# Element-wise transfers replaced by TensorE transposes, and two side streams with further waiting steps, in a two-layer hybrid decoder step

## Chip, core and metric

The kernel runs on one core of one Trainium2 chip. The metric is device time in microseconds (us) of one execution; the time before is 2325.03 us, the median of three runs.

## The reference

Two groups of tokens pass through a 2-layer decoder with shared weights: a prompt of 2048 tokens and 8 sample rows of one token each, all 1024 wide, in f32. A layer is

```
hn   = RMSNorm(x) * norm_w
proj = hn @ w_in                      # 1024 x 3336, split into 15 column groups
A retention      : r_q r_k r_v r_g    # 4 heads, state 64 x 64, rotary on q and k
B mLSTM          : m_q m_k m_v m_o m_g m_i m_f    # state c, n, m
C S5             : s_u s_g            # 16 groups, 64 complex states each, x_t = a x_(t-1) + B u_t
D memory attend  : a_q a_g            # 256 memory tokens
y    = x + concat(A, B, C, D, each times a SiLU gate) @ w_out
```

A final RMSNorm follows. The last states of A, B and C are outputs for both groups. For the S5 states these are `s5re_p`, `s5im_p` (16 x 64 per layer) of the prompt and `s5re_s`, `s5im_s` of the samples.

## The kernel before

**Units.** The 2048 tokens are cut into 4 units of 512 (UT), so there are 8 units, (layer, unit) from (0,0) to (1,3). `wstream` (L277) lists the work as weight groups: per unit 13 groups of 256 columns of w_in (`m_v` with 8 more), and the four output groups `out0` to `out3` of the unit before. The order is ORDER (L41): m_v, s_u, out0 to out3, m_k, m_q, m_o, a_q, r_k, r_v, r_q, s_g, a_g, m_g, r_g. In unit (0,1) the outputs stand behind a_q. Each f32 product is three float32r products (a value split into a high and a low part), so weights are loaded, split on ScalarE and on VectorE or GpSimd (`wsplit`, L345), and kept split in DRAM (`ws`) for the next units.

**Main stream and sides.** `group` (L449) is a Python generator for one weight group. It emits a piece of matmuls into a PSUM bank, evacuates it, and yields. At each yield `step_sides` (L1854) lets every side stream in `self.sides` emit up to its own next yield. So a bare `yield` in a side stream is a waiting step: its next instructions are emitted one main piece later. Tile's scheduler fixes each engine's order from this at build time; at run time an engine takes its instructions in that order. Almost all DMAs are issued on SyncE's queue by `dma` (L190), some on ScalarE's by `dmaa` (L193), where ScalarE's own later work stands behind them.

**Samples.** The 8 sample rows ride in unit 1 of each layer. Seven groups, FEAT (L37), are computed features by tokens: there the 8 sample columns are columns 512 to 519 of `hT`, a unit's 512 columns are cut into pieces of 260, and the result for the samples is 128 features by 8 rows. Lines 479 to 481 copy it to a small tile and store it transposed into `sproj`, a DRAM buffer of 8 rows by 3336, so each element is a run of 4 bytes. The other groups go through `sample_group` (L1538), which writes rows. After `r_g` the side stream `sample_layer` (L1577) reads `sproj` back in the layouts that each branch wants. `sample_s5` (L1773) loads the inputs of S5 transposed again, element by element (L1785).

**The other lines concerned.** `s5_pre` (L1112) prepares the S5 tables of a layer; it loads `s5_a_re` and `s5_a_im` transposed, each twice (L1122, L1123), and B in four arrangements (L1129). For layer 0 it starts with the kernel, for layer 1 in unit (0,2). `s_core` (L1321) is the S5 scan of a unit; in the last unit it stores the final state transposed (L1392). `m_gates` (L804) makes the mLSTM gates: after its transposes it copies RT (L857), waits one step, copies a part of RT (L862) and multiplies it on TensorE (L863), and then sets G_done, for which `m_core` waits. `sample_hn` (L1520) loads the norm weights, normalises the 8 sample rows (ScalarE, then some 12 small VectorE instructions) and transposes them on TensorE. It is called inline: before the main loop for layer 0 (L1924), and at `out3` of layer 0 for layer 1 (L1564).

Of the kernel before, what the change touches and what calls it, by code (L numbers as in the profile page):

```python
# [22 lines left out]
SG = 16  # L23
# [5 lines left out]
D_IN = 3336  # L29
# [4 lines left out]
NB = 8  # L34
# [84 lines left out]
class Builder:  # L119
# [93 lines left out]
    def setup(self):  # L213
        nc, I, cp = self.nc, self.I, self.cp
        c = lambda n, s, dt=F32: cp.tile(s, dt, name=n, tag=n)
        self.ident = c("ident", [128, 128])
        self.dma(self.ident, I["c_ident"])
        self.wstream()
        self.mem_load()
        self.wload(0)  # L220
        self.hnl = self.hn_load(0, 0)
        next(self.hnl)
        self.wload(1)
        self.maskb = c("maskb", [128, 512], BF16)
        self.identb = c("identb", [128, 128], BF16)
        mt = self.t2([128, 512])
        self.dma(mt, I["c_mask"])
        nc.vector.tensor_copy(self.maskb, mt)
        nc.vector.tensor_copy(self.identb, self.ident)
        self.Dt = c("Dt", [128, 2, 2, 128])  # L230
        self.dma(self.Dt, I["c_D"])
        self.vd = c("vd", [128, H])
        self.dma(self.vd, I["c_vd"])
        self.ropes = c("ropes", [128, 2, 16])
        self.dma(self.ropes, I["c_ropes"])
        self.smc = c("smc", [128, 4])
        self.dma(self.smc, I["c_sm"])
        self.e127 = c("e127", [128, 1])
        self.dma(self.e127, I["c_e127"])
        self.s32 = c("s32", [128, 32])  # L240
        self.dma(self.s32, I["c_s32"])
        self.s8 = c("s8", [128, 8])
        self.dma(self.s8, I["c_s8"])
        st = self.t2([128, H])
        self.dma(st, I["c_sel"])
        self.sel = c("sel", [128, H], F32R)
        nc.vector.tensor_copy(self.sel, st)
        zero = self.t2([128, 320])
        nc.vector.memset(zero, 0.0)
        self.ones = c("ones", [128, 1])  # L250
        nc.vector.memset(self.ones, 1.0)

        self.hT = [cp.tile([128, 8, UT + NB], F32R, name=f"hT{i}", tag=f"hT{i}") for i in range(2)]
        self.Sr = [c(f"Sr{i}", [128, 2, 128]) for i in range(3)]
        self.Cm = [c(f"Cm{i}", [128, 2, 130]) for i in range(3)]
        for t in self.Sr + self.Cm:
            nc.vector.memset(t, 0.0)
        self.mprev = c("mprev", [4, 8])
        self.hS = [c(f"hS{i}", [128, 8, 40], F32R) for i in range(2)]
        for i in range(2):  # L260
            nc.vector.tensor_copy(self.hS[i].rearrange("p a b -> p (a b)"), zero)

        T = self.T
        self.xd = [self.dram([T, D], f"xd{i}") for i in range(self.depth)]
        self.xsd = [self.dram([NB, D], f"xsd{i}") for i in range(self.depth)]
        self.sproj = [self.dram([NB, D_IN], f"sproj{i}") for i in range(self.depth)]
        self.smix = [self.dram([NB, D], f"smix{i}") for i in range(self.depth)]
        self.stab = []
        self.memd = []
        for l in range(self.depth):  # L270
            self.stab.append(dict(
                Wi=self.dram([128, SG, 128], f"Wi{l}"), TW=self.dram([128, 3, 1024], f"TW{l}"),
                CS=self.dram([128, 2, SG, 128], f"CS{l}"), Kd=self.dram([32, 16, 112], f"Kd{l}"), ab=self.dram([128, 3, SG], f"ab{l}"),
                C1=self.dram([128, SG, SC], f"C1{l}")))
            self.memd.append((self.dram([128, 2, MEM], f"mk{l}"), self.dram([128, 2, GW], f"mv{l}")))
# [173 lines left out]
    def group(self, i):  # L449
# [5 lines left out]
        if kind == "mem":  # L455
            self.mem_group(l, b, hi, lo)
            self.advance(i, 0)
            self.advance(i, 1)
            yield
        elif kind == "out":  # L460
            if self.sample_in_unit(kind, l, b):
                while not self.smix_done[l]:
                    self.step_sides()
                self.sample_group(i, l, g, hi, lo, kind)
            yield from self.group_out(i, l, b, g, hi, lo)
        elif g in FEAT:
            if g == "r_q":
                for m in range(2):
                    self.u["rq", m] = self.g4([128, 2, UT], n="rqt")
                    self.dmaa(self.u["rq", m], self.I["c_rq"][b, m])  # L470
            smp = self.sample_in_unit(kind, l, b)
            pieces = [(0, 260), (260, 520)] if smp else [(0, UT)]
            for m in range(2):
                for c0, c1 in pieces:
                    ps = self.feat_bank(m, hi, lo, slice(c0, c1))
                    c2 = min(c1, UT)
                    self.evac_f(l, b, g, m, ps[:, :c2 - c0], slice(c0, c2))
                    if c1 > UT:
                        o = self.sm([128, 16])[:, :NB]
                        self.nc.vector.tensor_copy(o, ps[:, c2 - c0:c1 - c0])  # L480
                        self.dma(AP(self.sproj[l], COL[g] + 128 * m, [[1, 128], [D_IN, NB]]), o)
                    if (c0, m) == (0, 0):
                        self.advance(i, 0)
                    if c1 >= UT and m == 1:
                        self.advance(i, 1)
                    yield
        else:
            if g == "m_v":
                jobs = [[t] for t in range(4)]
            else:  # L490
                jobs = [[0, 1], [2, 3]]
            n = 264 if g == "m_v" else 256
            for m, ts in enumerate(jobs):
                sls = [slice(t * 128, (t + 1) * 128) for t in ts]
                ps = self.tok_bank(sls, n, hi, lo, self.hslice)
                self.evac(l, b, g, m, ps)
                if m in (0, len(jobs) - 1):
                    self.advance(i, min(m, 1))
                if g == "r_g":
                    nxt = self.next_unit(l, b)  # L500
                    if nxt:
                        self.hn_T(2 * m)
                        self.hn_T(2 * m + 1)
                yield
# [299 lines left out]
    def m_gates(self, u, l, b):  # L804
# [48 lines left out]
        ps = self.bank()  # L853
# [3 lines left out]
        v.tensor_copy(RT, ps.rearrange("p (t q h) -> p t q h", t=NT, q=4)[:, :, :, 0:H])  # L857
        u["RT"] = RT
        yield
        pw = self.bank()  # L860
        ws = self.sm([128, 16])
        v.tensor_copy(ws.rearrange("p (t h) -> p t h", t=NT), RT[:, :, 1, :])  # L862
# [249 lines left out]
    def s5_pre(self, l):  # L1112
# [5 lines left out]
        packA = self.t2([128, 512], n="packA")  # L1118
        packC = self.t2([128, 2, SG, SC], n="packC")
        ar, ai, dt = S(), S(), S()  # L1120
        for h in range(2):
            self.dma(ar[64 * h:64 * h + 64], I["s5_a_re"][l].rearrange("g p -> p g"))  # L1122
            self.dma(ai[64 * h:64 * h + 64], I["s5_a_im"][l].rearrange("g p -> p g"))  # L1123
        self.dma(dt, AP(I["s5_log_dt"][l], 0, [[0, 128], [1, SG]]))
        Bst = P1([2, SG, SC], "Bst")
        for h in range(2):
            for w in range(2):
                src = I["s5_b_re" if h == w else "s5_b_im"][l]
                self.dma(Bst[64 * h:64 * h + 64, w], src.rearrange("g p c -> p g c"))  # L1129
        yield  # L1130
        yield
        self.pexp(dt, SG)
        mag, th, cs, sn, k, tmp, thl = S(), S(), S(), S(), S(), S(), S()
        v.tensor_tensor(mag, ar, dt, OP.mult)
# [186 lines left out]
    def s_core(self, u, l, b):  # L1321
# [66 lines left out]
        yield  # L1388
        yield
        if b == self.NU - 1:  # L1390
            for h, on in enumerate(("s5re_p", "s5im_p")):
                self.dma(self.O[on][l, 0].rearrange("g p -> p g"), self.xprev[64 * h:64 * h + 64])  # L1392
        gl = self.g4([128, 2, UT], n="gl")
        gh_, gl_ = [self.g4([128, 2, UT], F32R, n="gls") for _ in range(2)]
        for gh in range(2):
# [124 lines left out]
    def sample_hn(self, l, x=None):  # L1520

        if x is None:
            x = self.g4([128, D], n="xs")[:NB]
            self.dma(x, self.I["x_sample"].rearrange("b o d -> (b o) d"))
        w = self.bcrow(self.I["norm_w"][l], dma=self.dma)
        self.rms_rows([x], w[:NB], NB)
        self.sample_T(x, self.hS[0], True)

    def sample_T(self, x, dst, cols=False):
# [8 lines left out]
    def sample_group(self, i, l, g, hi, lo, kind):  # L1538
# [16 lines left out]
        else:  # L1555
# [5 lines left out]
            if g == 3:  # L1561
                if l + 1 < self.depth:
                    self.dma(self.xsd[l], self.xrow)
                    self.sample_hn(l + 1, self.xrow)  # L1564
                else:
                    w = self.bcrow(self.I["final_norm_w"])
                    self.rms_rows([self.xrow], w[:NB], NB)
                    self.dma(self.O["y_sample"].rearrange("b o d -> (b o) d"), self.xrow)

    def s_load(self, t, l, name, width, off=0, outer=True):  # L1570

# [201 lines left out]
    def sample_s5(self, l, lc):  # L1773
# [8 lines left out]

        uT = self.s64([128, 8, NB], n="suT")
        for pr in range(8):
            self.dma(uT[96:128, pr, :], AP(dr, COL["s_u"] + 32 * pr, [[1, 32], [D_IN, NB]]))  # L1785
        st = self.t1([128, 2, 128], n="sst")
        for w, nme in enumerate(("state_s5_re", "state_s5_im")):
            src = I[nme][l].rearrange("b g p -> (b g) p")
# [121 lines left out]
    def build(self):  # L1910
# [10 lines left out]
        for t in range(NT):  # L1921
            self.hn_T(t)
        if "nosample" not in self.dbg:
            self.sample_hn(0)  # L1924
        self.sides.append(self.pre(0))
        i = 0
        while i < len(self.wseq):
# [62 lines left out]
```

## Time and profile before

| what | before |
|---|---|
| median of 3 runs | 2325.03 us (2319.82 to 2328.7) |
| the profiled execution | 2328.93 us |
| its span, first to last instruction | 2327.1 us |
| mean granted TensorE clock | 0.962 |
| DMA packets | 392905, of them 115800 under 512 B |

The profile is of one execution. PE is TensorE's matmuls, PEld its weight loads, DVE VectorE, ACT ScalarE, POOL GpSimd, SP SyncE; `ACTq` and `SPq` are the queues of these engines, when they issue a DMA. L12 is line 12 of the kernel. A tile's name stands as output <- inputs. "idle before <- X" is the time that the engine stood before an instruction, and what ended it. A granted clock of 1 is 2.4 GHz, of 0.5 it is 1.2 GHz.

### The profile page before, as it was taken

Reading aid. Unit: us, or ns where it says so; the run is one execution under the profiler, and the core shown is the slowest. Engines: PE = TensorE matmul, PEld = TensorE weight load, DVE = VectorE, ACT = ScalarE, POOL = GpSimd, SP = SyncE. Lnnn points to the kernel's source line nnn. Section 1 sums busy time; section 2 is a strip of 40 time slices with the busy share of each in tenths; the row PEclk is TensorE's granted clock in tenths of the full one; section 3 lists DMA queues with packets and bytes.
Section 4 is the critical chain, followed back from the end, with each engine's and each line's share of the span. In section 5 each row is a group of like instructions: output and inputs, shape, how many; then the busy total and the mean of one; then the engine's idle time right before and its main releaser. Section 6 shows DMA issues by size and latency. Waiting matters only on the chain. (4 is left out here: it accounts for less than half of the span.)

```text
span 2327.1 us, 44458 instructions
## 1 busy us (share of the span) xinstructions
PE 2160.1 (93%) x16386; PEld 1991.0 (86%) x16386; DVE 1424.2 (61%) x3883; ACT 778.3 (33%) x1842; POOL 405.5 (17%) x435
## 2 busy tenths in 40 slices
PE   7889977899999999989899999898999899999998
PEld 6688967899997888888798989887899788888888
DVE  7787855535465687565944768355465466656463
ACT  4445422323223332134422454222331233312332
POOL 3343111111001113120202331110100001121011
PEclk9999988999999999989999999898999999999999
DMA  7878587978686656877568884996877776598634
GB/s 223 297 251 270 201 163 140 225 257 139 175 276 202 219 187 214 294 146 230 160 199 281 267 275 149 242 287 132 176 142 258 273 222 209 185 315 211 180 116 153
DMA packets 392905, 496.88 MB, mean 214 GB/s; under 512 B 115800, under 2 KB 216344, under 8 KB 392688
## 3 DMA queue, kind: packets, MB, share of 16 engines
q1 hardware_dynamic: 366848, 433.61, 64.3%
q10 hardware_dynamic: 25840, 60.43, 8.8%
q8 instruction: 129, 2.11, 0.4%
q14 instruction: 88, 0.72, 0.1%
HBM read 376.75 MB, written 118.21 MB: 213 GB/s over the span
## 5 line engine op out<-in xcount | busy, mean ns | idle before, releaser
L181 PE MATMUL pm<-hT,w 128*128 128x512 f32 (+1 forms) x3360 | 681.4, 358 | 9.2 <-ACT w L188 5.9
L181 PEld LDWEIGHTS pm<-hT,w 128*128 128x128 f32 x3360 | 550.7, 193 | 98.1 <-ACT w L188 6.5
L181 PE MATMUL pm<-w,hT 128*128 128x256 f32 (+1 forms) x4608 | 607.8, 288 | 12.8 <-DMA w<-ws 5.0
L181 PEld LDWEIGHTS pm<-w,hT 128*128 128x128 f32 x4608 | 574.1, 193 | 21.4 <-DMA w<-ws 7.2
L181 PE MATMUL pm<-w,mix 128*128 128x256 f32 x3072 | 379.8, 285 | 3.7 <-ACT w L188 2.1
L181 PEld LDWEIGHTS pm<-w,mix 128*128 128x128 f32 x3072 | 372.8, 192 | 4.9 <-ACT w L188 2.3
L366 POOL TENSOR_TENSOR w<-w,w 128x512 fp32r<-128x512 f32 (+1 forms) x76 | 110.0, 1448 | 370.4 <-ACT w L188 158.9
L188 ACT ACTIVATE w<-w 128x512 fp32r<-128x512 f32 (+1 forms) x152 | 95.0, 633 | 181.2 <-DMA w<-w_in 78.1
L1358 POOL TENSOR_TENSOR sA<-sy,sCS 128x512 f32<-128x512 f32 x32 | 53.0, 1658 | 363.1 <-DVE sy L1355 162.0
L366 DVE TENSOR_TENSOR w<-w,w 128x512 fp32r<-128x512 f32 (+1 forms) x76 | 54.6, 720 | 87.7 <-ACT w L188 73.2
L188 ACT ACTIVATE Pt<-ps,sm 128x256 f32<-128x256 f32 x128 | 58.9, 472 | 114.5 <-DVE sm L994 93.0
L1454 DVE TENSOR_TENSOR xr<-xr,pm 128x512 f32<-128x512 f32 x56 | 38.2, 684 | 78.2 <-PE pm L181 32.4
L188 ACT ACTIVATE sB<-ps 64x512 f32<-64x512 f32 x64 | 37.9, 592 | 107.9 <-DVE sy L1347 83.7
L1355 DVE TENSOR_TENSOR_SCAN sy<-ab,xprev,sy 128x128 f32<-128x128 f32 x128 | 57.3, 505 | 0.6
L1414 POOL TENSOR_TENSOR t<-t,s_g 128x512 f32<-128x512 f32 x16 | 25.4, 1584 | 175.2 <-DVE t L1412 83.7
L643 POOL TENSOR_TENSOR r_k<-rp 128x256 f32<-128x256 f32 x32 | 24.2, 759 | 181.8 <-DVE rp L641 160.3
L993 DVE TENSOR_REDUCE sm<-ps 128x2 f32<-128x512 f32 x64 | 42.3, 685 | 21.2 <-PE ps L181 20.9
L181 PE MATMUL ps<-X,sWi 128*128 128x128 f32 x256 | 38.6, 297 | 17.2 <-DMA sWi<-Wi 11.2
L588 POOL TENSOR_TENSOR r_qT<-rqs,rqs 128x512 f32<-128x512 f32 (+2 forms) x20 | 22.0, 1100 | 184.5 <-DVE rqs L587 100.3
L898 POOL TENSOR_TENSOR vw<-mv,RT 128x260 f32<-128x260 f32 x32 | 22.1, 699 | 178.5 <-DVE sm L1109 69.4
L181 PEld LDWEIGHTS ps<-X,sWi 128*128 128x128 f32 x256 | 33.1, 202 | 21.6 <-issue 21.5
L185 PE MATMUL ps<-ident,xt 128*128 128x128 f32 x256 | 38.2, 300 | 13.2 <-DVE xt L387 11.5
(434 smaller groups left out, 3308.5 us busy)
## 6 DMA issues: line engine op xcount, KB each, us to landing
w<-ws SPq DMA_DIRECT2D x768, 256.0 KB
ws<-w SPq DMA_DIRECT2D x256, 256.0 KB
w<-w_in SPq DMA_DIRECT2D x104, 256.0 KB
sCS<-CS SPq DMA_DIRECT2D x32, 512.0 KB
xd<-xr SPq DMA_DIRECT2D x56, 256.0 KB
w<-ws SPq DMA_DIRECT2D x48, 264.0 KB
sTW<-TW SPq DMA_DIRECT2D x32, 384.0 KB
xt<-x_prompt ACTq DMA_DIRECT2D x16, 512.0 KB
```

Of the source, the lines that this page charges most:

```text
L181: self.nc.tensor.matmul(out, lhsT, rhs, start=start, stop=stop, skip_group_check=skip)
L185: self.nc.tensor.transpose(out, in_, self.ident[:K, :K])
L188: self.nc.scalar.activation(out, in_, f, **kw)
L366: e.tensor_tensor(lo[q], r[q], hi[q].bitcast(F32), OP.subtract)
L588: self.nc.gpsimd.tensor_tensor(u["r_qT"][:, m, c], q, qs, OP.add)
L643: gp.tensor_tensor(dst[:, x, :], t1.rearrange("p h f -> p (h f)"), t2.rearrange("p h w f -> p (h w f)"), OP.add)
L898: gp.tensor_tensor(vw, mv[:, j], RT[:, j, 3, :, None].to_broadcast([128, H, 65]), OP.mult)
L993: v.tensor_reduce(mx[:, 2 * x:2 * x + 2], ps[x].rearrange("p (a m) -> p a m", a=2), AX.X, OP.max)
L1355: v.tensor_tensor_scan(t1[:, g], self.abt[:, 2, gg:gg + 1].to_broadcast([128, 128]), t1[:, g], self.xprev[:, gg:gg + 1], OP.mult, OP.add)
L1358: gp.tensor_tensor(A[:, :, 1:129], t1, Cs, OP.mult)
L1414: gp.tensor_tensor(zg.rearrange("p (j s) -> p j s", s=4), z.rearrange("p (s j) -> p j s", s=4), u["s_g", m].rearrange("p (j s) -> p j s", ...
L1454: v.tensor_tensor(xr, xr, ps.rearrange("p (t c) -> p t c", t=2), OP.add)
```

## The change

1. In unit 1 the sample columns of the 14 feature pieces are collected in one tile `sft` [128, 14, 8]. When the last is there, a new side stream `sample_feat` waits one step, transposes it in one TensorE instruction, and ScalarE copies the 112 rows; seven DMAs store them with runs of 512 bytes.
2. `sample_s5` copies its inputs on ScalarE from `sft` (8 copies of 32 x 8) in place of 8 loads.
3. `s5_pre` loads `s5_a_re`, `s5_a_im` by rows, four loads of 16 x 64, and transposes twice on TensorE; of the four loads of B two stay, and ScalarE makes the other two arrangements.
4. `s_core` transposes the final state and stores rows.
5. `m_gates` has one more `yield` behind RT.
6. `sample_hn` becomes a side stream with two waiting steps ahead of its transposes.

```
--- before.py
+++ after.py
@@ group
-                        o = self.sm([128, 16])[:, :NB]
-                        self.nc.vector.tensor_copy(o, ps[:, c2 - c0:c1 - c0])
-                        self.dma(AP(self.sproj[l], COL[g] + 128 * m, [[1, 128], [D_IN, NB]]), o)
+                        if "sft" not in self.u:
+                            self.u["sft"] = self.tb([128, 2 * len(FEAT), NB], "sft")
+                            self.u["sft_n"] = 0
+                        self.nc.vector.tensor_copy(self.u["sft"][:, 2 * FEAT.index(g) + m, :], ps[:, c2 - c0:c1 - c0])
+                        self.u["sft_n"] += 1
+                        if self.u["sft_n"] == 2 * len(FEAT):
+                            self.sides.append(self.sample_feat(l, self.u["sft"]))
@@ m_gates
         u["RT"] = RT
         yield
+        yield
         pw = self.bank()
@@ s5_pre
-        for h in range(2):
-            self.dma(ar[64 * h:64 * h + 64], I["s5_a_re"][l].rearrange("g p -> p g"))
-            self.dma(ai[64 * h:64 * h + 64], I["s5_a_im"][l].rearrange("g p -> p g"))
+        at = P1([2, 128], "at")[:SG]
+        for w, nme in enumerate(("s5_a_re", "s5_a_im")):
+            for h in range(2):
+                self.dma(at[:, w, 64 * h:64 * h + 64], I[nme][l])
...
-            for w in range(2):
-                src = I["s5_b_re" if h == w else "s5_b_im"][l]
-                self.dma(Bst[64 * h:64 * h + 64, w], src.rearrange("g p c -> p g c"))
-        yield
-        yield
+            self.dma(Bst[64 * h:64 * h + 64, 0], I[("s5_b_re", "s5_b_im")[h]][l].rearrange("g p c -> p g c"))
+        yield
+        yield
+        ps = self.bank()
+        for w in range(2):
+            self.tr(ps[:, SG * w:SG * w + SG], at[:, w])
+        v.tensor_copy(ar, ps[:, 0:SG])
+        v.tensor_copy(ai, ps[:, SG:2 * SG])
+        for h in range(2):
+            self.act(Bst[64 * h:64 * h + 64, 1], Bst[64 - 64 * h:128 - 64 * h, 0])
@@ s_core
+            ps = self.bank()
+            self.tr(ps[:SG, :128], self.xprev)
+            xo = self.t1([128, 128], n="xo")[:SG]
+            self.act(xo, ps[:SG, :128])
             for h, on in enumerate(("s5re_p", "s5im_p")):
-                self.dma(self.O[on][l, 0].rearrange("g p -> p g"), self.xprev[64 * h:64 * h + 64])
+                self.dma(self.O[on][l, 0], xo[:, 64 * h:64 * h + 64])
@@ sample_hn
         self.rms_rows([x], w[:NB], NB)
+        yield
+        yield
         self.sample_T(x, self.hS[0], True)
@@ sample_group
-                    self.sample_hn(l + 1, self.xrow)
+                    self.sides.append(self.sample_hn(l + 1, self.xrow))
@@
+    def sample_feat(self, l, sft):
+        self.sft[l] = sft
+        yield
+        n = 2 * len(FEAT) * NB
+        ps = self.bank()
+        self.tr(ps[:n, :128], sft.rearrange("p g b -> p (g b)"))
+        o = self.t1([128, 264], n="sfo")
+        self.act(o[:n, :128], ps[:n, :128])
+        for i, g in enumerate(FEAT):
+            self.dma(AP(self.sproj[l], COL[g], [[128, 2], [D_IN, NB], [1, 128]]), o[2 * NB * i:2 * NB * (i + 1), :128])
@@ sample_s5
-            self.dma(uT[96:128, pr, :], AP(dr, COL["s_u"] + 32 * pr, [[1, 32], [D_IN, NB]]))
+            self.act(uT[96:128, pr, :], self.sft[l][32 * (pr % 4):32 * (pr % 4) + 32, 2 * FEAT.index("s_u") + pr // 4, :])
@@ build
-            self.sample_hn(0)
+            self.sides.append(self.sample_hn(0))
```

## Rows read from the trace of the kernel before

**Rows 1.** The page, busy time, share of the span and instructions of each engine.

```profile
PE 2160.1 (93%) x16386; PEld 1991.0 (86%) x16386; DVE 1424.2 (61%) x3883; ACT 778.3 (33%) x1842; POOL 405.5 (17%) x435
```

**Rows 2.** Windows, by unit: us, busy PE PEld DVE ACT POOL, clock, DMA share, GB/s.

```profile
268.00:608.00 340.00, 298.10 (x2448) 286.27 (x2447) 181.05 (x452) 106.77 (x271) 48.20 (x46) 0.92 0.78 176
608.00:864.00 256.00, 248.97 (x1848) 226.83 (x1847) 159.99 (x522) 79.97 (x191) 27.44 (x39) 0.99 0.70 220
864.00:1149.00 285.00, 270.27 (x1970) 242.82 (x1969) 195.34 (x485) 92.44 (x212) 61.61 (x76) 0.96 0.71 213
1149.00:1423.00 274.00, 263.34 (x1959) 240.49 (x1959) 169.07 (x420) 104.61 (x239) 57.05 (x50) 0.98 0.73 237
1423.00:1732.00 309.00, 278.09 (x2321) 269.23 (x2320) 165.02 (x446) 99.23 (x249) 39.63 (x41) 0.93 0.82 192
1732.00:1984.00 252.00, 245.26 (x1830) 223.68 (x1829) 145.31 (x441) 73.18 (x182) 21.09 (x23) 0.99 0.71 234
```

**Rows 3.** DMA issues: tile, queue, count, KB each.

```profile
sproj<-sm SPq DMA_DIRECT2D x28, 4.0 KB
...
suT<-sproj SPq DMA_DIRECT2D x16, 1.0 KB
...
sm<-s_a_re SPq DMA_DIRECT2D x4, 4.0 KB
...
s5re_p<-xprev SPq DMA_DIRECT2D x2, 4.0 KB
```

**Rows 4.** Windows over four stretches behind such transfers, columns as in rows 2.

```profile
326.00:333.00 7.00, 0.98 (x9) 0.77 (x7) 0.00 (x0) 0.00 (x0) 0.00 (x0) 0.94 1.09 65
355.00:362.00 7.00, 4.93 (x48) 4.44 (x46) 3.10 (x8) 2.88 (x7) 0.00 (x0) 1.00 0.71 32
1562.00:1580.00 18.00, 18.00 (x146) 16.95 (x143) 10.80 (x31) 2.84 (x10) 1.25 (x3) 0.84 0.84 85
2115.00:2133.00 18.00, 18.00 (x115) 15.34 (x113) 14.80 (x41) 4.97 (x14) 2.80 (x4) 1.00 1.01 42
```

**Rows 5.** Timelines of SP, ACT and PE: start us, us, instruction, [idle before <- releaser].

```profile
321.85 0.82 SPq L191 DMA_DIRECT2D sproj<-sm  x1
...
330.60 2.63 ACTq L194 DMA_DIRECT2D X<-ud  x4
333.28 0.66 ACT L188 ACTIVATE mkT<-pm 128x260 f32<-128x260 f32 x2 [11.14 <-issue]
...
334.36 0.58 PE L181 MATMUL ps<-sm,e 128*128 128x16 f32 x2 [7.38 <-DVE sm L862]
```

**Rows 6.** PE's waits in unit (0,1): us in total, times, longest us.

```profile
PE ps L181 <- DMA sWi<-Wi: 6.6, 1, 6.6
...
PE ps L181 <- DMA sproj<-sm: 6.0, 1, 6.0
```

**Rows 7.** PE's waits in unit (1,1).

```profile
PE ps L181 <- issue: 13.4, 2, 8.9
PE ps L185 <- ACT rows L188: 7.4, 1, 7.4
```

**Rows 8.** PE's timeline at the sample rows' norm of layer 1.

```profile
1249.94 0.66 PE L185 MATMUL ps<-ident,xrow 8*128 8x8 f32 x8 [4.62 <-DVE xrow L387]
```

**Rows 9.** Timelines of PE and ACT near the start.

```profile
68.68 3.63 PE L181 MATMUL pm<-hT,w 128*128 128x512 f32 x9 [4.28 <-ACT w L188]
...
68.00 0.63 ACT L188 ACTIVATE w<-w 128x512 fp32r<-128x512 f32 x1 [6.09 <-DMA w<-w_in]
```

**Rows 10.** Timelines of SP and PE behind layer 1's stores of the final state.

```profile
2119.69 14.90 SPq L191 DMA_DIRECT2D w<-ws  x4
...
2138.22 4.01 PE L181 MATMUL pm<-w,hT 128*128 128x256 f32 x15 [1.13 <-DMA w<-ws]
```

**Rows 11.** Instructions nearest to the added ones: ns min/median/max, first and last start.

```profile
L185 PE MATMUL ps<-ident,mkT x64: 270/272/421, 104.0 to 2090.5; 128*128 128x128 f32 x64
...
L188 ACT ACTIVATE sm<-sB x64: 206/207/210, 268.7 to 2110.1; 64x4 f32<-64x4 f32 x64
```

**Rows 12.** PE's timeline: a main piece of 48 matmuls.

```profile
375.93 5.82 PE L181 MATMUL pm<-w,hT 128*128 128x256 f32 x48
```

More of the change, by code (lines that the diff above doesn't have):

```diff
@@ L268, in setup @@
         self.stab = []
+        self.sft = {}
         self.memd = []
```

## The prediction

> **What bounds the kernel now.** I first read the busy shares: TensorE works 93% of the span and no other engine above 61% [rows 1], so time can come from TensorE's idle stretches and from what a lower clock costs, little else. Then I cut the span at the first m_v matmul of each unit and compared units [rows 2]. Idle time is length minus busy PE; to it I add busy time times (1 - granted clock) as an estimate of what the lower clock costs. In order the six units give 41.9 + 23.8 = 65.7, 7.0 + 2.5 = 9.5, 14.7 + 10.8 = 25.5, 10.7 + 5.3 = 16.0, 30.9 + 19.5 = 50.4 and 6.7 + 2.5 = 9.2 us. The first and the fifth carry the sample columns; the other four lose 15.1 us on average. So the two sample units lose 50.6 + 35.3 = **86 us** more than a unit needs to. They also have the highest DMA shares at the lowest rates (0.78 and 0.82 at 176 and 192 GB/s, against 0.70 to 0.73 at 213 to 237): their DMA engines are busy with something that moves few bytes.
>
> What that is, the issue list shows: 28 stores of the sample columns of 4.0 KB each, in runs of 4 bytes, 1024 runs each [rows 3]. Behind them the queue nearly stands [rows 4]: in 7 us behind one store 32 GB/s pass, in 18 us behind three stores 85 GB/s, in 18 us behind the two stores of the final state 42 GB/s. So one store of 1024 elements takes 6 to 9 us of all the DMA engines, and 28 of them some 170 to 250 us of the queue that also brings weights and tables.
>
> How that reaches TensorE is seen once in full [rows 5]. A store is issued at 321.85. ScalarE, in order, wants to issue the loads of X, which need a transfer caught in the same traffic; it can at 330.60, and only then evacuates mkT, after 11.14 us idle. VectorE stands behind that, and TensorE waits 7.38 us for L862. Elsewhere in that unit TensorE waits 6.0 us with such a store as releaser and 6.6 us for a table [rows 6]; in the other, 13.4 us in two waits put down to issue, and 7.4 us for ScalarE [rows 7].
>
> **The change part by part.** The sum is made against the profiled execution, 2328.9 us; its span is 1.8 us less, and it stands 3.9 us above the median of the runs.
>
> *Sample columns (part 1).* All 28 element stores go; 14 stores in runs of 512 bytes come, 7 a layer. The VectorE copies stay the same number. Of the 86 us not all comes back: when the queue lets go, the next late thing decides (the exponentials on ScalarE, weight splits), as in units without samples, and some of the 86 us is the sample groups' own work. The bounds are a third, 29 us, if most waits find another releaser, and the whole 86 us. I take two thirds, **57 us**, nearer to the top, because the waits I could follow [rows 5 to 7] sit in or right behind slow stretches. Because the columns are now stored only after a_g, the last feature group, I looked at who reads them: sample_layer starts behind r_g, two groups later, and one such stretch of main work is four pieces of about 5.8 us [rows 12]. Its first loads wait on SP with the weight loads queued behind them; the cover of some 23 us is more than the 6 to 9 us that even an element store takes.
>
> *S5 inputs (part 2).* 16 element loads of 1.0 KB go [rows 3]; 16 ScalarE copies come, the nearest row 0.21 us [rows 11], 3.4 us in all on an engine busy 33%. I found no wait of TensorE on them: 0. If they stall it as the stores do, 86 / 28 = 3.1 us for 1024 runs, these 4096 runs bring 12 us; if the copies hold up ScalarE's other work they cost 3: bounds -3 and 12.
>
> *S5 tables (part 3).* Per layer four loads of 1024 elements and two of four loads of B go; four row loads, two transposes, two VectorE copies and two ScalarE copies come. In layer 0 the old loads stand ahead of the first weights of w_in; at 68 us ScalarE waits 6.09 us for w<-w_in and TensorE 4.28 us for ScalarE [rows 9]. I take **4 us**, bounds 0 (weights bound by the bytes ahead of them) and 9 (twice the wait, for the waits that follow). For a loss: the new transposes wait on TensorE for their loads, with all matmuls behind them; they are emitted two steps later, in which pieces of 5.8 us run, so I count none.
>
> *Final state (part 4).* In layer 1 SP is held 14.90 us over four weight loads behind the stores, and TensorE then waits for weights, the last time 1.13 us [rows 10], with slower matmuls after it. I take **4 us**, bounds 0 and 10.
>
> *m_gates (part 5).* The multiplication behind L862 comes one piece later in eight units, which gives VectorE 5.8 us more [rows 12]. Its 7.38 us wait is counted in the 86 already; **1 us** more, bounds 0 and 2. Behind the waiting step stands m_core, which waits for G_done; four output groups lie between in most units, so that cover hides it, and if it were gone, one piece a unit would be the cost.
>
> *Sample norm (part 6).* In layer 1 TensorE stands 4.62 us for the normalised rows [rows 8], and matmuls are slow after it. With the step behind two further pieces (11.6 us, against a chain of about 5 us) the wait goes: **6 us**, bounds 4 and 7. What moves: two loads on SP (rows and a 512 KB broadcast of the weights), one ScalarE, a dozen VectorE instructions, eight small transposes, the splits. The loads move by at most one piece past weight loads on SP; nothing reads the result before unit 1, hundreds of us later.
>
> *Added on TensorE:* per layer 2 + 1 + 1 transposes; 8 x 0.27 us [rows 11] = 2 us, **-2 us**.
>
> The sum is 57 + 4 + 4 + 1 + 6 - 2 = 70 us: 2328.9 - 70 = 2259 for a profiled execution, and 2325 - 70 = **2255 us** for the median. With all upper bounds 86 + 12 + 9 + 10 + 2 + 7 - 2 = 124, so 2201; with the lower ones 29 - 3 + 4 - 2 = 28, so 2297.
>
> **The rule weighed.** By the rows an element store costs the queue 6 to 9 us [rows 4]. The Trainium skill, "DMA: Bandwidth & Descriptors", section Bandwidth, gives a measured 4 KB transfer as 0.68 us, with about 10.5 ns for each of 64 packets. By that the 28 stores would be 19 us of the queue, an estimate from that page, and would hold up nobody; the rows contradict it for 1024 runs of 4 bytes, and I go by the rows.
>
> **Rivals.** *(a) The waits move on.* The queue is freed, but evacuation, weight splits or the extra matmuls of the sample groups (six groups of 16 in unit 1) keep TensorE waiting in the same places, and a fifth of the 86 us, 17 us, comes back. Then 17 + 6 + 4 - 2 = 25 us, 2300 us. For it: units without samples lose up to 25.5 us [rows 2]. Against it: their DMA rate is higher and three of the four lose 9 to 16 us. *(b) Element transfers cost little and the slow stretches have another cause*, such as dependent transfers waiting for one another. Then parts 1 to 4 give nothing, and parts 5 and 6 less the transposes give 1 + 6 - 2 = 5 us: 2320 us. Against it: slow stretches also follow the final state's stores, where no sample column moves [rows 4]. *(c) Slower: m_core ends the unit.* If the chain from G_done through m_core to the gates decides when out0 can start, the extra step costs a piece of 5.8 us in each of eight units, 46 us. It decides once more than half of the units end on that chain and the queue gives back under 25 us; with (b) it gives 2325 + 46 - 5 = 2366 us. Against it: m_g and r_g stand behind m_core in the order.
>
> **How the numbers follow.** Forecast 0.76 (2201 to 2297), (a) 0.14, (b) 0.06, (c) 0.04. The range takes the forecast without its last 11 us below, where all upper bounds would have to meet (0.04), and the near part of (a): **2212 to 2302**, leaving out about 0.2. A measurement of this kernel can tell 0.5%, 11.6 us, from no change; below 2313.4 lie the forecast and most of (a): faster 0.89; same is (b) and the edge of (a), 0.07; slower is (c), 0.04.
>
> **What would show it.** Right: the two sample units lose 15 to 35 us each in idle time and clock, their rate is above 200 GB/s, no 7 us stretch in them stays under 40 GB/s, the waits of rows 5 to 8 are gone, and packets fall by some 49,000 (40 x 1024 of stores and table loads in 4 bytes, 16 x 256 of S5 inputs, 4 x 1024 of B). Wrong: these units keep 50 us or more with the element packets gone (a); slow stretches remain where no element transfer is (b); or TensorE waits at out0 for mix tiles of the mLSTM (c). A queue that is free but waits of ScalarE and VectorE of the old size would fell the two thirds.

## The result, and the profile after

The changed kernel takes 2225.51 us (median of 4 runs, 2222.94 to 2231.72), beside 2326.75 us for the kernel before (4 runs). The ratio is 0.9574, with a 95% interval of 0.9544 to 0.9603: a gain of about 101 us, where 70 was forecast; the time lies inside the range of 2212 to 2302 us. The profiled execution took 2231.72 us, with a span of 2229.9 us and a mean granted clock of 0.978.

The page of the changed kernel, its busy shares and the line of its DMA packets:

```profile
PE 2129.9 (96%) x16394; PEld 1964.8 (88%) x16394; DVE 1428.1 (64%) x3887; ACT 784.5 (35%) x1866; POOL 404.3 (18%) x435
...
DMA packets 343430, 496.61 MB, mean 223 GB/s; under 512 B 66100, under 2 KB 166868, under 8 KB 343212
```

Against [rows 1] TensorE's share rises from 93% to 96% and its busy time falls by 30.2 us, although it has 8 instructions more: matmuls ran less often at the lower clock. The packets fell from 392905 by 49475, as forecast, at nearly the same bytes.

The windows by unit, cut at the first m_v matmul as in [rows 2] and with the same columns; the first and the fifth line are the sample units:

```profile
268.00:556.00 288.00, 280.69 (x2443) 270.82 (x2443) 179.81 (x450) 106.92 (x271) 48.01 (x46) 0.99 0.63 207
556.00:815.50 259.50, 252.05 (x1853) 228.72 (x1852) 161.20 (x524) 81.14 (x193) 28.85 (x40) 0.98 0.69 217
815.50:1100.50 285.00, 267.56 (x1968) 240.77 (x1966) 193.60 (x486) 93.80 (x221) 60.59 (x74) 0.97 0.69 215
1100.50:1373.00 272.50, 264.27 (x1958) 240.73 (x1956) 169.13 (x417) 104.26 (x239) 58.12 (x50) 0.97 0.72 236
1373.00:1638.00 265.00, 264.23 (x2323) 257.49 (x2322) 166.06 (x446) 98.63 (x250) 41.37 (x41) 1.00 0.66 224
1638.00:1889.00 251.00, 247.81 (x1836) 226.12 (x1835) 146.58 (x442) 73.67 (x182) 21.12 (x23) 0.99 0.72 235
```

The sample units went from 340.0 to 288.0 us and from 309.0 to 265.0 us: 52 + 44 = **96 us**. The four others went from 256 + 285 + 274 + 252 = 1067 to 259.5 + 285 + 272.5 + 251 = 1068 us. The span fell by 97.2 us, so within 2 us the whole gain of the profiled execution lies in the two sample units. Idle time in them is now 7.3 and 0.8 us, and the clock 0.99 and 1.00; by the prediction's estimate they lose 10.1 and 0.8 us.

TensorE's waits in unit (0,1), in us in total, times, longest, to be held against [rows 6]:

```profile
PE ps L181 <- DMA yd<-Y: 3.9, 1, 3.9
PE ps L181 <- DVE Cm L927: 1.0, 1, 1.0
```

The waits of 6 us and more are gone there, and so is the 7.38 us wait of [rows 5]. Unit (1,1), which had 13.4 and 7.4 us [rows 7], keeps 0.6 us as its longest.

### The profile page after: what moved, and what is told of

Same layout as the page of the kernel before. It is cut to its first block, busy times and chain, and to the rows that moved or that the text cites. A ratio compares the mean times of both kernels' runs of the same rounds, so it can differ in the third digit from the quotient of the medians.

```text
span 2229.9 us, 44441 instructions
## 1 busy us (share of the span) xinstructions
PE 2129.9 (96%) x16394; PEld 1964.8 (88%) x16394; DVE 1428.1 (64%) x3887; ACT 784.5 (35%) x1866; POOL 404.3 (18%) x435
## 2 busy tenths in 40 slices
DMA packets 343430, 496.61 MB, mean 223 GB/s; under 512 B 66100, under 2 KB 166868, under 8 KB 343212
## 5 line engine op out<-in xcount | busy, mean ns | idle before, releaser
L181 PEld LDWEIGHTS pm<-hT,w 128*128 128x128 f32 x3360 | 544.5, 190 | 97.5 <-DVE w L367 5.1
L181 PE MATMUL pm<-w,hT 128*128 128x256 f32 (+1 forms) x4608 | 601.2, 287 | 9.2 <-DVE w L367 3.6
L181 PEld LDWEIGHTS pm<-w,hT 128*128 128x128 f32 x4608 | 567.9, 191 | 17.1 <-ACT hT L188 5.1
L207 DVE TENSOR_TENSOR sm<-sm 128x8 f32<-128x8 f32 (+4 forms) x210 | 46.4, 222 | 4.8
## 6 DMA issues: line engine op xcount, KB each, us to landing
w<-ws SPq DMA_DIRECT2D x48, 264.0 KB
```

What stands on the lines that cost most here:

```text
L181: self.nc.tensor.matmul(out, lhsT, rhs, start=start, stop=stop, skip_group_check=skip)
L207: v.tensor_tensor(t, y, y, OP.mult)
```

## The experiments

The expectations name theories by a letter. A: the element stores stall the sample units, and the gain is theirs. F: the norm's waiting steps (part 6) only move its wait. G: the changed kernel loses time because the final state's tile holds a buffer. H: ScalarE, standing in order at its own loads, is the main way from the queue to TensorE. The kernel before took longer beside these runs (medians of 2366.63, 2370.87 and 2367.65 us) than beside the first, so each ratio is against the runs of before on its own chip.

### The sample columns alone, and everything but them

The first kernel is the one before with parts 1 and 2; the second is the changed kernel with these two undone:

```
-  self.dma(AP(self.sproj[l], COL[g] + 128 * m, [[1, 128], [D_IN, NB]]), o)
+  self.nc.vector.tensor_copy(self.u["sft"][:, 2 * FEAT.index(g) + m, :], ps[:, c2 - c0:c1 - c0])
...
-  self.dma(uT[96:128, pr, :], AP(dr, COL["s_u"] + 32 * pr, ...))
+  self.act(uT[96:128, pr, :], self.sft[l][...])
```

> The kernel before with parts 1 and 2 alone (sample columns through the tile sft, S5 inputs copied from it). Theory A, the 28 element stores hold up the queue and with it the two sample units: these units shorten by the 51 and 44 us that they shortened in the changed kernel, so about 2326 - 95 = 2231 us (2222 to 2245). Rival B, the gain is shared by the other parts: clearly over 2260 us. Rival C, all the parts are needed together: 2290 us or more.

> The changed kernel with parts 1 and 2 undone (28 element stores and 16 element loads as before, parts 3 to 6 kept). Theory A: parts 3 to 6 are worth little, 2310 to 2328 us, with units (0,1) and (1,1) again at about 340 and 309 us. Rival B, parts 3 to 6 carry a third of the gain: about 2290 us. Had my sum been right, 2326 - 13 = 2313 us.

Parts 1 and 2 alone: 2233.89 us, ratio 0.9431 (0.9389 to 0.9472). Parts 3 to 6 alone: 2375.27 us, ratio 1.0025 (0.9988 to 1.0062). The windows of the two sample units, first of parts 1 and 2 alone:

```profile
268.00:555.00 287.00, 280.60 (x2448) 271.24 (x2446) 181.24 (x452) 107.61 (x272) 47.63 (x46) 0.99 0.65 209
1369.00:1633.00 264.00, 264.00 (x2320) 257.57 (x2319) 165.85 (x446) 98.22 (x249) 39.98 (x41) 1.00 0.67 226
```

and of parts 3 to 6 alone:

```profile
268.50:620.50 352.00, 298.43 (x2442) 286.73 (x2441) 180.31 (x452) 106.00 (x270) 47.89 (x46) 0.90 0.80 170
1445.00:1777.50 332.50, 283.18 (x2322) 273.71 (x2320) 166.31 (x446) 98.87 (x249) 39.63 (x41) 0.90 0.83 179
```

With parts 1 and 2 alone the units are as short as in the changed kernel (287 and 264 us); without them they stay long, and the other four parts together bring nothing that can be measured. The 13 us that the sum gave them would be a ratio of 0.9944, outside the interval. Part 2 has no share in the two units: the S5 loads that it replaces are issued from 940 to 959 us and from 2050 to 2071 us in the kernel before, in units (0,3) and (1,3). The two kernels ran on one chip, so the split is not one between chips.

### Element stores where there were none

The changed kernel, with 14 stores of the old form into a scratch buffer in unit 2 of each layer:

```
+  if b == 2:
+      o = self.sm([128, 16])[:, :NB]
+      self.nc.vector.tensor_copy(o, ps[:, 0:NB])
+      self.dma(AP(self.sxtra[l], COL[g] + 128 * m, [[1, 128], [D_IN, NB]]), o)
```

> The changed kernel plus 14 element stores in unit 2 of each layer, 8 prompt columns of each feature piece to a scratch buffer, with their VectorE copies: the same 28 stores in units that have no sample work. Theory A, the stores themselves hold up the queue: units (0,2) and (1,2), 259 and 251 us in the changed kernel, get 35 to 55 us longer each, 2295 to 2335 us in all. Rival D, only the sample units suffer, since their sample groups and pieces of 260 leave no slack: under 15 us in all, 2240 us. A store by the page's price of 0.68 us would add under 5 us.

It took 2409.72 us (2407.28 to 2411.85), ratio 1.0171 (1.0128 to 1.0215). The windows of its unit 2 in both layers, which are the second and the sixth line of the changed kernel's windows above:

```profile
555.00:901.00 346.00, 271.73 (x1854) 245.29 (x1852) 164.03 (x541) 81.30 (x194) 30.27 (x41) 0.87 0.72 166
1723.00:2062.00 339.00, 267.96 (x1834) 241.66 (x1833) 146.23 (x450) 72.58 (x182) 22.55 (x23) 0.88 0.76 174
```

These units, which had carried no samples' columns, went from 259.5 to 346 and from 251 to 339 us: 86.5 and 88 us for 14 stores each, **6.2 us a store**. The kernel with parts 1 and 2 alone, on the chip of this run, takes 260.5 and 254.0 us for them, so the difference is not one between chips. Each added store brings a copy of 128 x 8 on VectorE, which the sample units keep in the changed kernel without being long. So the stores alone make such units, samples or not. It is more than expected. The route can be followed in the timelines of SyncE, ScalarE, VectorE and TensorE at the longest wait of its first unit 2:

```profile
827.99 13.45 SPq L191 DMA_DIRECT2D w<-ws  x5
841.49 0.89 SPq L191 DMA_DIRECT2D smn<-state_mlstm_n  x2
842.50 0.39 SPq L191 DMA_DIRECT2D sxtra<-sm  x1
...
848.68 0.28 DVE L1719 SCALAR_TENSOR_TENSOR smn<-smn,sex,smk 128x64 f32<-128x64 f32 x1 [25.08 <-DMA smn<-state_mlstm_n]
...
849.90 0.58 PE L181 MATMUL ps<-kh,aq 128*128 128x256 f32 x1 [18.32 <-DVE Sr L708]
```

and the window in which SyncE and VectorE stand:

```profile
819.00:842.00 23.00, 12.59 (x81) 9.41 (x77) 2.43 (x4) 1.01 (x2) 3.46 (x5) 0.80 0.90 106
```

The DMA engines are busy 0.90 of that window at 106 GB/s, where the same unit of the changed kernel has 0.69 at 217 GB/s. SyncE's queue is held 13.45 us over five weight loads; the small load of a sample state behind them lands late; VectorE, in order, stands 25.08 us for it; behind it stands L708, for which TensorE waits 18.32 us. In [rows 5] the chain ran over ScalarE and a load of X. The engine between differs, the pattern of the two is one: a load of a side stream, late in a queue that stands, holds an engine on which the main stream depends.

### The same bytes in runs of 32 bytes

The kernel before, with its 28 stores and their tiles, but 8 elements to a run:

```
-  self.dma(AP(self.sproj[l], COL[g] + 128 * m, [[1, 128], [D_IN, NB]]), o)
+  self.dma(AP(self.sxtra[l], NB * (COL[g] + 128 * m), [[NB, 128], [1, NB]]), o)
```

> The kernel before with the same 28 stores of 4 KB in the same places, but to a scratch buffer in 128 runs of 32 bytes in place of 1024 runs of 4. The sample rows' feature columns are left out: the rows of m_v stand in their place, by seven row stores a layer. Theory A, the number of runs is the price: 2326 - 95 + some = 2235 to 2255 us. Rival E, the number of stores, their waits or the small tile that they hold are the price: 2310 to 2330 us.

It took 2249.42 us (2249.25 to 2251.21), ratio 0.9497 (0.9449 to 0.9545). Its sample units:

```profile
269.00:557.50 288.50, 281.96 (x2441) 271.92 (x2440) 179.66 (x450) 106.76 (x269) 48.33 (x46) 0.99 0.65 208
1373.00:1648.00 275.00, 268.05 (x2320) 260.74 (x2319) 165.38 (x446) 98.27 (x248) 39.20 (x41) 0.99 0.64 217
```

Its line of DMA packets, and under it those of the run with the 28 added element stores:

```profile
DMA packets 368041, 497.00 MB, mean 221 GB/s; under 512 B 90824, under 2 KB 191480, under 8 KB 367824
...
DMA packets 372550, 496.73 MB, mean 206 GB/s; under 512 B 95220, under 2 KB 195988, under 8 KB 372332
```

The runs can be counted there. The added element stores bring 372550 - 343430 = 29120 packets over the changed kernel, 1040 each, a little over their 1024 runs; with runs of 32 bytes the packets are 24864 fewer than in the kernel before, 888 fewer for each of the 28 stores.

Still 28 stores of 4 KB, issued behind the same pieces, and 288.5 and 275 us instead of 352.0 and 332.5 in the run with element stores on this chip. Against the 287 and 264 us without them that is 1.5 + 11 = 12.5 us for 28, under 0.5 us a store. The 12.5 us also hold the seven row stores a layer that stand in for the columns. So neither the number of stores, nor their bytes, nor their issue is the price: the 1024 runs of 4 bytes are. Whether it is their number or their length cannot be told apart at equal bytes, and the 32-byte runs also lie next to each other in DRAM.

### The loads off ScalarE's queue

The kernel before, with its loads of X (L1333) and yT (L1387) issued on SyncE's queue:

```
-  self.dmaa(X[32 * s:32 * s + 32], ...)
+  self.dma(X[32 * s:32 * s + 32], ...)
...
-  self.dmaa(yT[:, gh], ...)
+  self.dma(yT[:, gh], ...)
```

> The kernel before, with the element stores, and only the loads of X and yT issued from SyncE's queue in place of ScalarE's. Theory H, the stores reach TensorE mostly through ScalarE, which stands at those issues with its evacuations and exponentials behind them: 20 to 40 us faster than the kernel before. Rival, tables and weights in the slow queue are late in any case (and SyncE then stands at those issues, with weight loads behind it): no change within 10 us, or slower.

2357.61 us, ratio 0.9953 (0.9923 to 0.9984): some 10 us, so H falls as the main way. TensorE's longest waits in its unit (0,1), in us in total, times, longest:

```profile
PE ps L181 <- DMA X<-ud: 17.8, 1, 17.8
PE ps L181 <- DMA sWi<-Wi: 8.9, 1, 8.9
PE ps L181 <- DVE PT L1017: 8.5, 1, 8.5
```

ScalarE no longer stands at X, and TensorE waits for X itself. In this run too the wait went to the next transfer that was late.

### The other parts, each undone in the changed kernel

The changed kernel once more, for the chip of two of these runs:

> The changed kernel once more, beside the three that follow, so that they are compared on one chip. All theories: 2220 to 2240 us, whatever the kernel before takes there; it and a kernel with the element stores differ from call to call, those without them should not.

2233.45 us (2230.63 to 2238.27), ratio 0.9435 (0.94 to 0.947).

Part 6 undone, the norm inline again:

```
-        yield
-        yield
         self.sample_T(x, self.hS[0], True)
...
-  self.sides.append(self.sample_hn(l + 1, self.xrow))
+  self.sample_hn(l + 1, self.xrow)
...
-  self.sides.append(self.sample_hn(0))
+  self.sample_hn(0)
```

> The changed kernel with part 6 undone: the sample rows' norm inline again. My prediction counted 6 us for part 6, so 6 us slower than the changed kernel. Theory F, the wait only moved (4.62 us before, 5.38 us after at the transposes of xrow, since a weight split that waits for its weights stands in VectorE's order inside the norm's chain): within 3 us of the changed kernel.

2234.87 us (2233.26 to 2237.78), 1.4 us above the run above, within the scatter. The place of [rows 8] in the changed kernel (timelines of ScalarE, VectorE and TensorE) shows why:

```profile
1207.05 0.63 ACT L188 ACTIVATE w<-w 128x512 fp32r<-128x512 f32 x1 [7.87 <-DMA w<-w_in]
...
1207.71 0.69 DVE L367 TENSOR_TENSOR w<-w,w 128x512 fp32r<-128x512 f32 x1 [4.72 <-ACT w L188]
...
1211.54 1.27 DVE L388 SCALAR_TENSOR_TENSOR xrow<-xrow,sm,bcrow 8x1024 f32<-8x1024 f32 x1
...
1212.87 1.02 PE L185 MATMUL ps<-ident,xrow 8*128 8x8 f32 x8 [5.38 <-DVE xrow L388]
```

A new weight arrives at 1207; ScalarE and then VectorE wait for it, and in VectorE's order its split stands ahead of the norm's last step. TensorE waits 5.38 us where it had waited 4.62. On this chip it waits 7.7 us with the norm inline and 6.0 us with the two steps; over all the runs here it is 3.3 to 7.7 us inline and 4.1 to 6.2 us with two steps. The wait stays, and F holds.

Part 4 undone, and part 4 kept with its tile from another pool:

```
-  xo = self.t1([128, 128], n="xo")[:SG]
-  self.act(xo, ps[:SG, :128])
   for h, on in enumerate(("s5re_p", "s5im_p")):
-      self.dma(self.O[on][l, 0], xo[:, 64 * h:64 * h + 64])
+      xo = self.s64([128, 64], n="xo")[:SG]
+      self.act(xo, ps[:SG, 64 * h:64 * h + 64])
+      self.dma(self.O[on][l, 0], xo)
```

> The changed kernel with part 4 undone: the final S5 state stored by elements again. My prediction counted 4 us for part 4: 4 us slower. Theory G, part 4 took away a slow stretch behind the stores and put in a new wait, since its tile xo holds one of three buffers that cst needs (TensorE waits 1.23 us and 4.72 us for cst at L972): those two waits go, slow stretches of 10 to 18 us behind the stores come back, in all within 5 us of the changed kernel.

> The changed kernel with xo taken from another pool (s64, two halves, two small ScalarE copies), so that cst does not wait for the stores of the state. Theory G: the waits for cst, 1.23 and 4.72 us, go, with the half clock behind the second, 5 to 10 us faster than the changed kernel. Rival: cst waits for something else that is late then, and nothing changes.

Undone: 2239.08 us (2233.02 to 2243.95), 5.6 us above the changed kernel of that chip, with ranges that overlap, so part 4 as it was built is worth nothing that can be told from scatter. With the other pool: **2224.04 us** (2221.14 to 2226.84), 9.4 us below it and 15.0 us below the run with part 4 undone, with ranges apart from both; ratio to before 0.9397 (0.9357 to 0.9437). The cause, first in the changed kernel (the run beside it), timelines of ScalarE, SyncE, VectorE and TensorE:

```profile
2065.89 0.25 ACT L188 ACTIVATE xo<-ps 16x128 f32<-16x128 f32 x1
2071.88 0.34 SPq L191 DMA_DIRECT2D s5re_p<-xo  x1
2072.44 0.34 SPq L191 DMA_DIRECT2D s5im_p<-xo  x1
2077.82 0.39 DVE L972 COPY cst<-Cm 64x64 f32<-64x64 f32 x2 [9.58 <-DMA s5im_p<-xo]
...
2078.36 0.39 PE L185 MATMUL ps<-ident,cst 128*64 128x128 f32 x1 [6.40 <-DVE cst L972]
```

and the same copy and transpose with the other pool:

```profile
2058.55 0.27 PE L185 MATMUL ps<-ident,cst 128*64 128x128 f32 x1
...
2058.86 0.39 DVE L972 COPY cst<-Cm 64x64 f32<-64x64 f32 x2
```

`xo` is ready at 2065.89, but SyncE issues its stores only 6 us later, and until they land it keeps a buffer of the pool from which the mLSTM's `cst` comes too. VectorE stands 9.58 us for that buffer and TensorE 6.40 us. In the pool `s64` no copy and no transpose of `cst` waits for `xo`. The two units with the store of a final state, (0,3) and (1,3) with what follows, are where the time goes, first in the changed kernel, then with the other pool (columns as in [rows 2]):

```profile
817.70:1103.20 285.50, 267.72 (x1967) 240.91 (x1965) 193.00 (x486) 93.69 (x221) 60.41 (x74) 0.97 0.69 214
1893.50:2236.50 343.00, 316.75 (x2426) 290.20 (x2424) 196.79 (x522) 96.74 (x260) 57.05 (x51) 0.98 0.60 194
...
814.20:1093.70 279.50, 266.72 (x1967) 240.53 (x1965) 191.96 (x481) 93.69 (x221) 61.96 (x74) 0.98 0.69 216
1882.00:2219.40 337.40, 319.37 (x2426) 293.31 (x2424) 196.45 (x522) 96.45 (x261) 56.99 (x51) 0.97 0.60 197
```

They are 6.0 and 5.6 us shorter, which is 11.6 of the 17.1 us between the two profiled executions; the rest is spread over the other units. G is borne out for the pool: part 4 brought in a stall of `cst`, and without it storing the state by rows is worth 15.0 us on this chip.

Part 3 undone, the element loads of the tables again, and part 5 undone, one waiting step less:

```
-  self.dma(at[:, w, 64 * h:64 * h + 64], I[nme][l])
+  self.dma(ar[64 * h:64 * h + 64], I["s5_a_re"][l].rearrange("g p -> p g"))
...
```

```
         u["RT"] = RT
         yield
-        yield
```

> The changed kernel with part 3 undone (the S5 parameters loaded by elements again, B in four loads). My prediction counted 4 us: 4 us slower than the changed kernel, 2230 to 2245. Theory K, the start is bound by bytes and by VectorE, and in unit (0,2) those loads stand in a stretch with slack: within 3 us at the start; what is lost is in unit (0,2), where the six loads of layer 1 fall.

> The changed kernel with part 5 undone (one waiting step less behind RT). My prediction counted 1 us. Theory L, the step moves the multiplication behind other work of VectorE and the wait stays (1.54 and 2.77 us in the changed kernel, 7.38 and 1.01 before): within 4 us of the changed kernel.

Part 3 undone: 2238.64 us (2232.48 to 2245.55), ratio 0.9453 (0.941 to 0.9497). Part 5 undone: 2229.1 us (2224.43 to 2232.36), ratio 0.9406 (0.9374 to 0.9438). The changed kernel was not run on this chip, and both intervals overlap the 0.9435 of the other: neither part can be told from nothing. Against each other the two are 9.5 us apart, with ranges that do not quite meet, so part 3 may be worth more than part 5. That difference does not stand where part 3's loads are: unit (0,1) begins at 266.8 us with part 3 undone, within the 262.4 to 269.2 us of the kernels that have it, and unit (0,2), where the loads of layer 1 fall, takes 258.7 us against 258.6 with part 5 undone. K's loss in unit (0,2) is not seen. As to L, TensorE's wait for the copy behind the step, first in the changed kernel beside the runs above, then with part 5 undone (whole span, in us in total, times, longest):

```profile
PE ps L181 <- DVE sm L868: 5.6, 3, 2.8
...
PE ps L181 <- DVE sm L867: 0.3, 1, 0.3
```

In all the kernels without element stores of the sample columns it is 4.3 to 8.6 us in total with the step and 0.3 to 2.5 us without it. The wait does not only stay; it is longer with the step.

### A version with further waiting steps

The changed kernel with the other pool for `xo`, six waiting steps ahead of the norm's transposes and a third in the first phase of m_gates, except in unit (0,0):

```
-        yield
-        yield
+        for _ in range(6):
+            yield
         self.sample_T(x, self.hS[0], True)
...
+        if (l, b) != (0, 0):
+            yield
```

> The changed kernel with xo from the other pool, six waiting steps in place of two ahead of the sample norm's transposes, and a third waiting step ahead of the gates' transposes except in unit (0,0). Theory F: the waits for xrow (5.38 us) and for the gates' input (3.25 and 3.08 us) go with the half clock behind them, 10 to 20 us faster than the changed kernel, so 2205 to 2220 us. Rival: later steps only meet other late work, no gain over the kernel with xo alone.

2232.03 us (2224.32 to 2234.34), ratio 0.9414 (0.938 to 0.9448), no better than the 0.9397 of the pool alone, nor than the 2229.1 us of part 5 undone on the same chip. TensorE at the multiplication of m_gates, which stands behind the gates' transposes, and at the norm's transposes:

```profile
892.34 0.40 PE L181 MATMUL ps<-sm,e 128*128 128x16 f32 x2 [3.52 <-DVE sm L870]
...
1232.67 0.66 PE L185 MATMUL ps<-ident,xrow 8*128 8x8 f32 x8 [1.11 <-ACT E L188]
...
1958.83 0.61 PE L181 MATMUL ps<-sm,e 128*128 128x16 f32 x2 [3.84 <-DVE sm L870]
```

Both waits that the steps were aimed at went: the norm's is down to 1.11 us, and at the gates' transposes, where the changed kernel had 3.25 and 3.08 us, none is left. At the multiplication behind them TensorE waits 3.52 and 3.84 us, against 2.80 and 1.50 us in the changed kernel beside the earlier runs. The time shows no gain, so the rival is borne out. This version also has `xo` in the other pool and no wait for `cst`, and is not faster than part 5 undone, which has that wait; so the 9.4 us of the pool are shown on one chip only. The lowest ratio is that of the changed kernel with `xo` in the other pool, with an interval that overlaps those of part 5 undone and of this version.

## Why the prediction was right in direction, and short in size

- **The bound, and its cause.** Right: the excess of the sample units came from the element stores. The two kernels with and without parts 1 and 2 separate it, the run with stores in unit 2 makes it anew, and the stores in runs of 32 bytes leave only the 1024 short runs as cause. Rivals (a) and (b) fall with these. Rival (c) falls too. In the page of the changed kernel the output matmuls have 0.9 us of TensorE's idle time ahead of them in the whole span, 0.6 us of it for a mix tile; and without the extra step the kernel took 2229.1 us, not 46 us less:

```profile
L181 PE MATMUL pm<-w,mix 128*128 128x256 f32 x3072 | 376.5, 283 | 0.9 <-ACT mix L188 0.6
```

- **The sample columns (part 1): the term that was mis-sized.** I took 57 of a bound of 86 us; it brought about 96. Two steps failed. The two thirds assumed that late work elsewhere and the samples' own work would keep a third of the loss. They did not: the units lose 10.1 and 0.8 us in idle time and clock, where 15 to 35 us each were expected. And the 86 was no upper bound, since it granted a sample unit the 15.1 us that the four other units lose on average. Those lose them partly to things of their own, such as the norm of layer 1 in unit (1,0), which a sample unit does not have. Why a sample unit then has even less idle time than the best of them, 0.8 us against 3.2, was not tried; that the extra pieces of the samples give late work time is an argument only.
- **The rule weighed.** The prediction priced a store by its bytes. By the Trainium skill, "DMA: Bandwidth & Descriptors", section Bandwidth, 28 stores of 4 KB were 19 us of the queue, an estimate. The units with added stores became 86.5 + 88 = 174.5 us longer for 28, nine times that. But that price is for 64 packets, as the prediction quotes it, and each of these stores is 1040. At the 10.5 ns a packet of the same section of the Trainium skill, given there for loads issued from GpSimd, a store would be 10.9 us, an estimate, against the 6 to 9 us that the prediction read from [rows 4]. So the prediction was wrong to say that the rows contradict the Trainium skill for 1024 runs: they contradict a price carried over by bytes, and the price by packets comes near.
- **S5 inputs (part 2)** were not tried apart from part 1. The run with stores of 32 bytes keeps these loads; there unit (0,3) takes 280.9 us and everything from unit (1,3) on 347.1 us, against 278.5 and 345.5 us with parts 1 and 2 alone on the same chip. That is 4 us together, from one profile each, inside the bounds of -3 and 12.
- **S5 tables (part 3), 4 us.** The step failed where it took a late first weight for a late matmul. TensorE's wait of [rows 9] shrank, but the time came back within 25 us, as TensorE's timeline near the start shows, first behind the 4.28 us before, then in the changed kernel:

```profile
83.70 1.19 PE L181 MATMUL pm<-hT,w 128*128 128x512 f32 x4 [1.61 <-ACT w L188]
88.08 7.27 PE L181 MATMUL pm<-hT,w 128*128 128x512 f32 x20 [3.19 <-DVE w L366]
...
65.35 3.98 PE L181 MATMUL pm<-hT,w 128*128 128x512 f32 x16 [1.54 <-ACT w L188]
79.97 1.19 PE L181 MATMUL pm<-hT,w 128*128 128x512 f32 x4 [2.74 <-ACT w L188]
85.87 6.34 PE L181 MATMUL pm<-hT,w 128*128 128x512 f32 x20 [4.72 <-DVE w L367]
```

The 4.28 us became 1.54, but the two waits behind it grew: 4.28 + 1.61 + 3.19 = 9.1 us before, 1.54 + 2.74 + 4.72 = 9.0 us after. Unit (0,1) begins at 267.9 us, before at 268.5. With part 3 undone in the changed kernel the first wait is absent altogether, so it was not the element loads alone that made it.
- **Final state (part 4), 4 us.** Part 4 undone was 5.6 us slower, of the forecast size but with ranges that overlap. The step that failed is that I counted the new tile at nothing and did not look at who else takes from its pool: its wait cost 9.4 us. With the tile in the other pool, part 4 is worth 15.0 us, more than my upper bound of 10.
- **m_gates (part 5), 1 us.** The 7.38 us of the sample unit are gone without the step too, in the kernel with parts 1 and 2 alone, so the stores had made them. Elsewhere the step made the wait longer, as shown above; in the time neither can be seen.
- **Sample norm (part 6), 6 us.** I counted pieces of TensorE's work against the length of the chain, and left out what the build order puts into the chain. A weight split that waits for its DMA stands in VectorE's order before the norm's last step, and two pieces later it still does. With six pieces the wait was 1.11 us, and the time no shorter.
- **Two signs of the list failed.** The wait of [rows 8] stayed, as told under part 6. "No 7 us stretch under 40 GB/s" fails in the changed kernel in stretches where nothing is wrong, such as these two windows (columns as in [rows 2]):

```profile
520.00:527.00 7.00, 7.00 (x61) 7.00 (x60) 5.70 (x14) 3.58 (x7) 2.62 (x2) 1.00 0.03 4
...
1527.00:1534.00 7.00, 7.00 (x62) 7.00 (x61) 6.00 (x15) 0.63 (x1) 1.47 (x2) 1.00 0.00 0
```

The rate is low since nothing is in transfer: the DMA share is 0.03 and 0.00, and TensorE is busy throughout. A stalled queue is a low rate at a high share, as in [rows 4].

## What to carry to other kernels

Count a store's runs before its bytes: 4 KB in 1024 runs of 4 bytes cost a unit of this kernel 3.1 to 6.2 us, and the same 4 KB in 128 runs of 32 bytes under 0.5. What other units lose on average is no floor for a stalled one, for they have stalls of their own. When a store is moved to a new tile, look at who shares the tile's pool, because here the buffer was held until the store had landed.

## What was not expected of the hardware

- The price of element stores is not one number. The kernel before took 2319.82 to 2328.7 us in the first runs and 2349.26 to 2384.49 us beside the experiments, while the changed kernel went only from 2222.94 to 2231.72 to 2230.63 to 2238.27 us. So nearly all of the difference, about 40 us against 8, goes with the element transfers. Most of it lies in the sample units: with parts 1 and 2 undone they took 352.0 and 332.5 us, 35.5 us more than in the first profile. What makes the stores dearer in some runs was not found.
- The same 14 stores cost 52 and 44 us in the sample units of the first profile, 3.1 to 3.7 us each, and 6.2 us each in unit 2. Part of it is the dearer store of those runs: on that chip the sample units with element stores were 352.0 - 287.0 = 65 and 332.5 - 264.0 = 68.5 us longer than without, 4.6 to 4.9 us a store. The rest, where in a unit the stores fall, stays open.
